# Second half's low weight parts by rows in two buffers; the first residue's tables in the weights' raw buffer

## The chip, the cores and the metric

The kernel runs on one core of a Trainium2 chip. The metric is the device time of one execution in microseconds (us); lower is better. The engines are TensorE (PE, and PEld for its weight loads), VectorE (DVE), ScalarE (ACT), GpSimd (POOL) and SyncE (SP, which here only issues DMAs).

## The reference

One block of a network on 2048 tokens of 1024 channels: a normalisation, a projection, a mixer, and a mixture of experts. The mixer's columns are half a long convolution done by Fourier transforms and half a two-dimensional Fourier transform. The part around the change:

```python
def fourier_mixer(u):
    B, L, _ = u.shape
    ug = u.astype(jnp.float32).reshape(B, L, N_FOURIER_GROUPS, HEAD_DIM)
    y = jnp.fft.fftn(ug, axes=(1, 3), norm='ortho').real
    return y.reshape(B, L, D_FOURIER)
...
    k_f = jnp.fft.rfft(k, n=2 * L, axis=0)
    u_f = jnp.fft.rfft(u, n=2 * L, axis=1)
    return jnp.fft.irfft(u_f * k_f[None], n=2 * L, axis=1)[:, :L]
```

## The kernel before

Products in float32 are made of three products of shorter numbers: each operand is cut into a high and a low part, and high by high, high by low and low by high are summed. The high part is a rounded copy (made on ScalarE), the low part is the operand minus the high part (made on VectorE).

The change lies in one stage, between about 400 and 620 us. Two kinds of work are mixed there.

**Fourier columns.** The 512 Fourier columns of the projection are made in two halves of 256 columns (h = 0 and 1). `fourier(h, i, ...)` makes the tile of 128 tokens number i of a half: 24 matmuls of 256 columns, three for each of the eight blocks d of 128 input channels. The normalised tokens, cut, are `hhi` and `hlo`, and stay in SBUF; the half's weights, cut, are `wh` and `wl`. 16 tiles by two halves by 24 are 768 matmuls. `fweights(h)` loads the half's weights from `Wp` by groups g of 128 columns into the raw buffer (tag `wraw`, one buffer, 4 KB of each partition) and cuts them with `cutg`. `wh` has two buffers (tag `whl`), `wl` one.

**Residues.** The long convolution's spectra are multiplied residue by residue: 32 calls of `residue(n)`. Each loads two tiles (`yl`, from `YK` and `YZ`), cuts them (`yh` on ACT; the low part of the first on POOL, of the second on DVE), makes the products K and U with the tables `sk` and `su`, multiplies them (`ks`, `t1`, `t2` on DVE), cuts the product (`ph` on ACT, `pl` on DVE), makes `zp` with the table `si` and stores it. That is 9 matmuls of 512 columns (12 for residue 0, which has tables of its own). Residues are counted from 0 here.

The calls are written one after the other (six Fourier tiles, six residues, and then a loop over h and i with residues between), and a scheduler decides the order on each engine. Each engine works its list off in that order. After the last tile of the second half the sums and differences of mirrored rows (`pair`, `fold`) and the next transforms (`bins`) follow; `h5` and `mid` are one row of 512 numbers for the middle frequency, `r0` the first rows for `reverse`.

Of the kernel before, what the change touches and what calls it, by code (L numbers as in the profile page):

```python
# [9 lines left out]
F32 = mybir.dt.float32  # L10
F32R = mybir.dt.float32r
# [192 lines left out]
def build(tc, I, out, dbg=None, upto=99):  # L204
# [4 lines left out]
    with es:  # L209
# [65 lines left out]
        with ExitStack() as e1, ExitStack() as e2:  # L275
# [388 lines left out]
            def fweights(h):  # L664

                wh = wp.tile([P, 8, 256], F32R, tag="whl", bufs=2, name="wh")
                wl = wx.tile([P, 8, 256], F32R, tag="wl", bufs=1, name="wl")
                for g in range(2):
                    wr = wp.tile([P, 8, P], F32, tag="wraw", bufs=1, name="wr")
                    S.dma_start(wr, Wp[2 * h + g])  # L670
                    cutg(wh[:, :, P * g:P * g + P], wl[:, :, P * g:P * g + P], wr)
                fw[h] = wh, wl

            def fourier(h, i, wh, wl, pm, dst=None):
# [3 lines left out]
                for d in range(8):  # L678
                    for a, b in ((hhi, wh), (hhi, wl), (hlo, wh)):
                        T.matmul(pm, a[q][:, d, P * o:P * o + P], b[:, d, :], start=n == 0, stop=n == 23)  # L680
                        n += 1
# [3 lines left out]
                if h and i in (12, 4):  # L685

                    rt = wx.tile([P, 256], F32, tag="rt", bufs=2, name="rt")
                    A.copy(rt, pm)
                    A.copy(h5[i // 12][:, 256:512], pm[0:1])
                    rts[i // 12] = rt  # L690
                    return
# [31 lines left out]
            ufirst(15)  # L723
            wh, wl = fw.pop(0)
            for i in range(NFIRST):
# [25 lines left out]
            def prod(o, w, xh, xl):  # L751

                for n, (a, b) in enumerate(((0, xh), (0, xl), (1, xh))):
                    T.matmul(o, w(a), b, start=n == 0, stop=n == 2)

            def residue(n):
# [6 lines left out]
                if n == 0:  # L763

                    for x in range(2):
                        prod(kp[x], lambda a: sk[:, r, a, P * x:P * x + P], kh, kl)
                    for x in range(2):
                        prod(up[x], lambda a: su[:, r, a, 64 - 64 * x:192 - 64 * x], uh, ul)
                    for x in range(2):
# [3 lines left out]
                else:  # L773

                    kp, up = kp[0], up[0]
                    prod(kp, lambda a: sk[:, r, a, 64:192], kh, kl)
                    prod(up, lambda a: su[:, r, a, 64:192], uh, ul)
                    lo, hi = slice(0, 64), slice(64, P)
# [11 lines left out]
                zp = ps.tile([P, DH], F32, tag="Z", bufs=2, name="zp")  # L790
                prod(zp, lambda a: si[:, r, a, :], ph, pl)
                zs = fp.tile([P, DH], F32, tag="zs", bufs=2, name="zs")
# [5 lines left out]
            def j0(i, h):  # L798
                return res < min(NT * h + i + 8, 32)
# [21 lines left out]

            rts, r0, h5 = {}, {}, {}

            def reverse(k):
# [48 lines left out]
            for h in range(2):  # L873
                if h:
                    wh, wl = fw.pop(h)
                for i in range(NT):
# [7 lines left out]
                    if h and i in (13, 14):  # L884
                        reverse(i - 13)
                    while j0(i, h):
                        residue(res)
                        res += 1
                        if res == 32:
# [14 lines left out]

                            x = wp.tile([P, 2, 512], F32, tag="wraw", bufs=1, name="h5")
                            for k in range(2):
                                h5[k] = x[0:1, k]
                                S.dma_start(h5[k][:, 0:256], RM[1 - k][3][0:1, 0:256])
                            lg = gp.tile([P, NT, 36], F32, name="lg")
                            lst = gp.tile([P, 2, 5, NE], F32, name="lst")  # L910
                            x = lg.rearrange("p a b -> p (a b)")
                            for k in range(2):
                                r0[k] = x[0:1, 256 * k:256 * k + 256]
                            jm = lst.rearrange("p a b c -> p (a b c)")[:, 0:P]
# [84 lines left out]
        with ExitStack() as e3:  # L999
# [82 lines left out]
            with tc.tile_pool(name="fo", bufs=1, side="right", reuse_waits="tile") as fo:  # L1082
# [8 lines left out]

                mid = fo.tile([1, 512], F32, name="mid")
                V.tensor_tensor(v4(mid[:, 0:264]), v4(h5[0])[:, :, 0:66], v4(h5[1])[:, :, 0:66], op=ALU.add)
                V.tensor_tensor(v4(mid[:, 264:512]), v4(h5[0])[:, :, 66:128], v4(h5[1])[:, :, 66:128], op=ALU.subtract)

# [899 lines left out]
```

## Time and profile before

| | us |
|---|---|
| median of 3 runs (lowest, highest) | 1671.64 (1668.62, 1673.2) |
| the profiled execution: time, span | 1675.47, 1673.7 |
| PE busy in the span | 1574.7 (94%) |
| DVE busy | 1192.6 (71%) |
| ACT busy | 1031.0 (62%) |
| POOL busy | 438.7 (26%) |

The span is what the hardware profiler saw of one execution; the time has what lies around it too. The busy time of PE counts pipelined matmuls whose ends are modelled, so where it works back to back the distance from start to start says more than the duration. The granted clock of TensorE is a share of full speed: 1.00 is 2.4 GHz, 0.50 is 1.2 GHz.

### The profile page before, as it was taken

The page shows a single profiled execution, that of the slowest core. Times are in us where ns is not written, and L with a number is a line of the kernel's source. Part 1 is how long each engine was busy: PE and PEld are TensorE (multiplying, and loading weights), DVE is VectorE, ACT ScalarE, POOL GpSimd, SP SyncE. Part 2 cuts the span into 40 slices and gives each one's busy share as a digit, 9 for nine tenths or more (in the row PEclk, how much of TensorE's full clock was granted, in tenths as well). Part 3 has the DMA queues.
Part 4 walks back from the last instruction along what each step waited for, and adds up shares of the span by engine and source line. Part 5 has one row for each costly group of instructions (what it writes and reads, how often), then busy time and mean ns, then how long its engine had stood idle before and what let it go on. Part 6 is the DMA issues. An engine that isn't in the chain of part 4 may idle for free.

```text
span 1673.7 us, 27233 instructions
## 1 busy us (share of the span) xinstructions
PE 1574.7 (94%) x8995; PEld 1200.8 (72%) x8995; DVE 1192.6 (71%) x2162; ACT 1031.0 (62%) x1746; POOL 438.7 (26%) x515
## 2 busy tenths in 40 slices
PE   7999999999998999999999999999999999999992
PEld 5767776778887787876666567777777777777740
DVE  7667756533499966555877877888878888888825
ACT  8445667555698844414444467777777777777732
POOL 0202444332233220103434331222222222221112
PEclk9999999999998999999999999999999999999996
DMA  7245677699765587668778689999999999999997
GB/s 265 66 133 156 191 214 217 189 312 256 212 197 189 176 257 232 203 222 229 230 225 320 227 315 337 337 353 361 343 325 338 351 369 340 333 340 349 378 383 281
DMA packets 202447, 449.77 MB, mean 269 GB/s; under 512 B 27037, under 2 KB 83066, under 8 KB 201280
## 3 DMA queue, kind: packets, MB, share of 16 engines
q1 hardware_dynamic: 129176, 316.25, 53.5%
q0 software_dynamic: 39568, 106.07, 22.4%
q10 hardware_dynamic: 33560, 25.69, 4.7%
q8 instruction: 72, 1.18, 0.3%
q14 instruction: 71, 0.58, 0.1%
HBM read 346.05 MB, written 103.17 MB: 268 GB/s over the span
## 4 chain that ended last, share of the span: by engine, by line
PE 73%; DVE 11%; ACT 5%; DMA 4%; issue 3%; POOL 1%; ACTq 0%; DVEq 0%; POOLq 0%; SPq 0%
PE pa L1722 20%; PE py L1815 10%; PE psm L323 9%; PE psd L1055 8%; PE po L1738 4%; PE pm L680 3%; PE po L1754 2%; PE pstr L1685 2%; PE pa L1719 1%; DMA xt<-in_x 1%; POOL acc L513 1%; PE psEO L1075 1%; PE psm L680 1%; PE pstr L1779 1%; PE pseo L1138 1%
## 5 line engine op out<-in xcount | busy, mean ns | idle before, releaser
L1538 DVE TENSOR_TENSOR l<-w,h 128x1024 fp32r<-128x1024 f32 x352 | 425.7, 1223 | 80.0 <-ACT h L1537 60.4
L1537 ACT CAST h<-w 128x1024 fp32r<-128x1024 f32 x352 | 368.9, 1049 | 106.9 <-PE pa L1722 75.2
L323 PE MATMUL psm<-hhi,wt 128*128 128x512 f32 x768 | 249.9, 396 | 0.7 <-ACT hhi L425 0.5
L1722 PE MATMUL pa<-h,xh 128*128 128x512 f32 x464 | 185.6, 400 | 0.2 <-issue 0.2
L1722 PE MATMUL pa<-l,xh 128*128 128x512 f32 x464 | 181.9, 392 | 0.0
L1722 PE MATMUL pa<-h,xl 128*128 128x512 f32 x464 | 181.6, 391 | 0.0
L323 PEld LDWEIGHTS psm<-hhi,wt 128*128 128x128 f32 x768 | 144.7, 189 | 35.9 <-issue 4.0
L323 PE MATMUL psm<-hlo,wt 128*128 128x512 f32 x384 | 151.7, 395 | 0.4 <-DVE hlo L426 0.2
L987 POOL DMA_INDIRECT xg<-XR,gia x30 | 45.9, 1529 | 295.0 <-PE pstr L1685 154.9
L1722 PEld LDWEIGHTS pa<-h,xh 128*128 128x128 f32 x464 | 87.0, 188 | 30.9 <-issue 12.0
L1722 PEld LDWEIGHTS pa<-h,xl 128*128 128x128 f32 x464 | 87.1, 188 | 20.2 <-DVE xl L1690 0.4
L1722 PEld LDWEIGHTS pa<-l,xh 128*128 128x128 f32 x464 | 87.1, 188 | 18.4 <-issue 0.4
L1815 PE MATMUL py<-l,sh 128*128 128x512 f32 x240 | 98.6, 411 | 0.0
L1815 PE MATMUL py<-h,sh 128*128 128x512 f32 x240 | 97.6, 407 | 0.7 <-ACT sh L1783 0.7
L1815 PE MATMUL py<-h,sl 128*128 128x512 f32 x240 | 96.3, 401 | 0.0
L323 PEld LDWEIGHTS psm<-hlo,wt 128*128 128x128 f32 x384 | 72.8, 189 | 16.6 <-DVE hlo L426 1.0
L1758 POOL DMA_INDIRECT X<-yo,sib x18 | 37.2, 2064 | 166.0 <-DVE l L1538 110.9
L748 POOL TENSOR_TENSOR yl<-yl,yh 128x512 fp32r<-128x512 f32 x32 | 48.6, 1522 | 108.2 <-ACT yh L747 82.8
L1738 PE MATMUL po<-w,xot 128*32 128x256 f32 x1152 | 66.9, 381 | 0.0
L513 POOL TENSOR_TENSOR acc<-ab,acc 128x512 f32<-128x512 f32 x32 | 48.2, 1507 | 69.0 <-ACT ab L512 67.8
L347 ACT COPY u<-psm 128x512 f32<-128x512 f32 x48 | 28.1, 586 | 53.0 <-PE psm L323 52.7
L680 PE MATMUL pm<-wh,hhi 128*128 128x256 f32 x208 | 59.9, 289 | 0.8 <-ACT wh L309 0.8
(495 smaller groups left out, 3655.8 us busy)
## 6 DMA issues: line engine op xcount, KB each, us to landing
w<-in_w_gate SPq DMA_DIRECT2D x128, 512.0 KB
w<-in_w_up SPq DMA_DIRECT2D x128, 512.0 KB
w<-in_w_down SPq DMA_DIRECT2D x120, 512.0 KB
xt<-in_x SPq DMA_DIRECT2D x31, 512.0 KB
de<-in_c_decay SPq DMA_DIRECT2D x32, 256.0 KB
YK<-yk ACTq DMA_DIRECT2D x32, 256.0 KB
z<-zT POOLq DMA_DIRECT2D x32, 256.0 KB, 5.9
YZ<-yz SPq DMA_DIRECT2D x64, 128.0 KB
```

Source lines behind the costliest of these rows:

```text
L323: T.matmul(pm, wt[:, a, d, :], b[q][:, d, :], start=n == 0, stop=n == 23)
L513: G.tensor_tensor(KS["acc"], ab, KS["acc"], op=ALU.add)
L680: T.matmul(pm, a[q][:, d, P * o:P * o + P], b[:, d, :], start=n == 0, stop=n == 23)
L748: e.tensor_tensor(yl, y, yh, op=ALU.subtract)
L987: G.indirect_dma_start(xg_[e], None, XR, bass.IndirectOffsetOnAxis(ap=ga[:, e:e + 1], axis=0))
L1055: T.matmul(pd, a[:, c, :], b[:, c, 512 * h:512 * h + 512], start=n == 0, stop=n == 11)
L1537: cuts.append(A.copy(h, raws[n]))
L1538: V.tensor_tensor(l, raws[n], h, op=ALU.subtract)
L1722: T.matmul(pa[m], x[:, 4 * k + c, :], y[:, f], start=d == 0 and q == 0, stop=d == 7 and q == 2)
L1738: T.matmul(po_[e][32 * j:32 * j + 32, 256 * m:256 * m + 256], xoT[e][:, b % 2, 2 * k + b // 2, :], w[:, 256 * j:256 * j + 256], start=b == ...
L1758: G.indirect_dma_start(X4, bass.IndirectOffsetOnAxis(ap=sib[:, d:d + 1], axis=0), yo, None, compute_op=ALU.add)
L1815: T.matmul(py[i], x[:, c, :], y[:, f], start=c == 0 and q == 0, stop=c == 3 and q == 2)
```

## The change

- `fweights(h)` loads the weights by rows (blocks d 0 to 3, then 4 to 7, of both column groups) and no longer by column groups: four DMAs of 256 KB in place of two of 512 KB. High parts: the same 16 casts. Low parts: blocks 0 to 3 go into a buffer `wl` that now has two (4 KB each), and are made with the load; blocks 4 to 7 go into one buffer `wm` (4 KB), and are made by `rest()`, which runs where the half begins. The low parts' memory grows from 8 to 12 KB of each partition.
- The tables of residue 0 (`t0`) lie in the weights' raw buffer until residue 0 is done; those of the other residues have half-size tiles. Three table DMAs on POOL's queue become nine, five of them into `t0`.
- `cs1` (tables of the next stage) takes the raw buffer after the weights; `h5` and `r0` take a buffer of `wl`.
- `mid` is made in two steps per half (`middle`), in the memory of `lg`, and no longer after the stage.

```diff
@@ -664,20 +664,41 @@
                 wh = wp.tile([P, 8, 256], F32R, tag="whl", bufs=2, name="wh")
-                wl = wx.tile([P, 8, 256], F32R, tag="wl", bufs=1, name="wl")
-                for g in range(2):
-                    wr = wp.tile([P, 8, P], F32, tag="wraw", bufs=1, name="wr")
-                    S.dma_start(wr, Wp[2 * h + g])
-                    cutg(wh[:, :, P * g:P * g + P], wl[:, :, P * g:P * g + P], wr)
-                fw[h] = wh, wl
+
+                wls = [wx.tile([P, 4, 256], F32R, tag="wl", bufs=2, name="wl")]
+
+                def low(j):
+                    for d in range(4):
+                        for g in range(2):
+                            sl = slice(P * g, P * g + P)
+                            V.scalar_tensor_tensor(wls[j][:, d, sl], wr[:, g, d, :], g1[:, 4 * j + d:4 * j + d + 1],
+                                                   wh[:, 4 * j + d, sl], op0=ALU.mult, op1=ALU.subtract)
+
+                for j in range(2):
+                    wr = wp.tile([P, 2, 4, P], F32, tag="wraw", bufs=1, name="wr")
+                    for g in range(2):
+                        S.dma_start(wr[:, g], Wp[2 * h + g][:, 4 * j:4 * j + 4, :])
+                    for d in range(4):
+                        for g in range(2):
+                            A.activation(wh[:, 4 * j + d, P * g:P * g + P], wr[:, g, d, :], AF.Copy,
+                                         scale=g1[:, 4 * j + d:4 * j + d + 1])
+                    if j == 0:
+                        low(0)
+
+                def rest():
+                    wls.append(wx.tile([P, 4, 256], F32R, tag="wm", bufs=1, name="wm"))
+                    low(1)
+                    return wh, wls
+
+                fw[h] = rest
...
@@ -733,11 +754,17 @@
-            su = fp.tile([P, 2, 2, 192], F32R, name="su")
-            sk = fp.tile([P, 2, 2, 256], F32R, name="sk")
-            si = fp.tile([P, 2, 2, P], F32R, name="si")
-            for x, n in ((su, "c_su"), (sk, "c_sk"), (si, "c_si")):
-                G.dma_start(x, I[n].rearrange("x p h c -> p x h c"))
+
+            t0 = wp.tile([P, 1024], F32R, tag="wraw", bufs=1, name="t0")
+            su = [[t0[:, 192 * a:192 * a + 192] for a in range(2)]]
+            sk = [[t0[:, 384 + 256 * a:640 + 256 * a] for a in range(2)]]
+            si = [[t0[:, 896:1024], fp.tile([P, P], F32R, name="si0")]]
+            for x, n, w in ((su, "c_su", 192), (sk, "c_sk", 256), (si, "c_si", P)):
+                y = fp.tile([P, 2, w], F32R, name=n)
+                G.dma_start(y, I[n][1])
+                for a in range(2):
+                    G.dma_start(x[0][a], I[n][0, :, a])
+                x.append([y[:, a] for a in range(2)])
...
+            def middle(h):
+                x, y = (h5[k].rearrange("p (g c) -> p g c", g=2) for k in range(2))
+                g = slice(2 * h, 2 * h + 2)
+                V.tensor_tensor(v4(mid[:, 0:264])[:, g], x[:, :, 0:66], y[:, :, 0:66], op=ALU.add)
+                V.tensor_tensor(v4(mid[:, 264:512])[:, g], x[:, :, 66:128], y[:, :, 66:128], op=ALU.subtract)
...
                 if h:
-                    wh, wl = fw.pop(h)
+                    wh, wl = fw.pop(h)()
...
+                    if h and i == 14:
+                        middle(1)
...
-                            css = {1: [fq.tile([P, 2, 2, 2, P], F32R, name="cs1")]}
+                            css = {1: [wp.tile([P, 2, 2, 2, P], F32R, tag="wraw", bufs=1, name="cs1")]}
...
-                            x = wp.tile([P, 2, 512], F32, tag="wraw", bufs=1, name="h5")
+                            x = wx.tile([P, 4, 256], F32, tag="wl", bufs=2, name="h5")
```

The scheduler's lists move in three places. The number after a name is the buffer's, not part of the code.

**VectorE, where the second half's low parts are cut.** Before (`wl` of the second half from its two raw loads, among the operations of residues 16 and 17):

```order
L782 TENSOR_TENSOR ks_5314<-U_5313,ks_5314 128x512
L310 SCALAR_TENSOR_TENSOR wl_4938<-wr_4939,vecs_89,wh_4937 128x128 x8
L789 TENSOR_TENSOR pl_5264<-ks_5249,ph_5263 128x512
L783 SCALAR_TENSOR_TENSOR ks_5314<-U_5313,ks_5314 64x512
L748 TENSOR_TENSOR yl_5438<-yl_5438,yh_5437 128x512
L784 TENSOR_TENSOR ks_5314<-U_5313,ks_5314 64x512
L782 TENSOR_TENSOR ks_5379<-U_5378,ks_5379 128x512
L785 TENSOR_TENSOR ks_5314<-ks_5314 128x512
L783 SCALAR_TENSOR_TENSOR ks_5379<-U_5378,ks_5379 64x512
L310 SCALAR_TENSOR_TENSOR wl_4938<-wr_4957,vecs_89,wh_4937 128x128 x4
L784 TENSOR_TENSOR ks_5379<-U_5378,ks_5379 64x512
L310 SCALAR_TENSOR_TENSOR wl_4938<-wr_4957,vecs_89,wh_4937 128x128 x4
```

After the change, at about the same place (`wm`, from residue 19 on):

```order
L674 SCALAR_TENSOR_TENSOR wm_5672<-wr_4969,vecs_89,wh_4948 128x128
L816 TENSOR_TENSOR pl_5464<-ks_5449,ph_5463 128x512
L811 TENSOR_TENSOR ks_5515<-U_5514,ks_5515 64x512
L674 SCALAR_TENSOR_TENSOR wm_5672<-wr_4969,vecs_89,wh_4948 128x128
L812 TENSOR_TENSOR ks_5515<-ks_5515 128x512
L809 TENSOR_TENSOR ks_5581<-U_5580,ks_5581 128x512
L810 SCALAR_TENSOR_TENSOR ks_5581<-U_5580,ks_5581 64x512
L816 TENSOR_TENSOR pl_5530<-ks_5515,ph_5529 128x512
L811 TENSOR_TENSOR ks_5581<-U_5580,ks_5581 64x512
L674 SCALAR_TENSOR_TENSOR wm_5672<-wr_4969,vecs_89,wh_4948 128x128
L812 TENSOR_TENSOR ks_5581<-ks_5581 128x512
L674 SCALAR_TENSOR_TENSOR wm_5672<-wr_4969,vecs_89,wh_4948 128x128 x2
```

The block of eight and the two of four are gone: eight cuts (`wl`) now stand singly among residues 3 to 11, eight (`wm`) among residues 19 to 22.

**ScalarE, where the second half's high parts are cut.** Before, the first eight stand ahead of the residues (the other eight in one block at residue 18):

```order
L309 ACTIVATE wh_4937<-wr_4939,vecs_89 128x128 x6
L694 COPY rt_4354<-psm_4329 128x256
L309 ACTIVATE wh_4937<-wr_4939,vecs_89 128x128
L694 COPY rt_4382<-psm_4357 128x256
L747 CAST yh_4487<-yl_4488 128x512
```

After the change none stands there; the first two are among the casts of residue 4 and the copies of residue 3:

```order
L774 CAST yh_4615<-yl_4616 128x512
L774 CAST yh_4620<-yl_4621 128x512
L774 CAST yh_4652<-yl_4653 128x512
L815 CAST ph_4567<-ks_4553 128x512
L774 CAST yh_4657<-yl_4658 128x512
L683 ACTIVATE wh_4948<-wr_4950,vecs_89 128x128 x2
L807 COPY ks_4627<-K_4625 64x512
```

All 16 of the second half now stand among residues 3 to 12. Their first load stands on SP's list behind the loads of residue 4 and waits until residue 0 has left the raw buffer.

**TensorE, residues 4 to 7** (`pm` is a Fourier tile). Before:

```order
L754 MATMUL K_4725<-yh_4715,sk_4482 128x512
L754 MATMUL K_4725<-yl_4716,sk_4482 128x512
L754 MATMUL K_4725<-yh_4715,sk_4482 128x512
L754 MATMUL zp_4634<-pl_4631,si_4483 128x512
L754 MATMUL zp_4634<-ph_4630,si_4483 128x512
L680 MATMUL pm_5144<-wl_3994,hhi2_117 128x256
L680 MATMUL pm_5144<-wh_3993,hlo2_121 128x256
L680 MATMUL pm_5144<-wh_3993,hhi2_117 128x256
```

After the change:

```order
L781 MATMUL K_4773<-yh_4763,c_sk_4490 128x512
L781 MATMUL K_4773<-yl_4764,c_sk_4490 128x512
L781 MATMUL K_4773<-yh_4763,c_sk_4490 128x512
L781 MATMUL zp_4682<-ph_4678,c_si_4494 128x512
L781 MATMUL zp_4682<-pl_4679,c_si_4494 128x512
L781 MATMUL zp_4682<-ph_4678,c_si_4494 128x512
L781 MATMUL U_4774<-yh_4768,c_su_4486 128x512
L781 MATMUL U_4774<-yl_4769,c_su_4486 128x512
```

No Fourier matmul stands between the residues' there any more. Counted over the whole list, the 768 Fourier matmuls stand so (from the end of the `zp` of one residue to that of another):

| Fourier matmuls | before | after |
|---|---|---|
| up to the end of residue 0 | 152 | 152 |
| residues 1 to 3 | 44 | 40 |
| residues 4 to 7 | 63 | 0 |
| residues 8 to 16 (residue 8, residue 9) | 125 (14, 15) | 148 (15, 11) |
| residues 17 to 22 | 96 | 93 |
| residues 23 to 31 | 172 | 218 |
| behind residue 31 | 116 | 117 |
| behind residue 28 | 185 | 214 |
| residue matmuls behind the end of residue 28 | 15 | 21 |

The lists of TensorE after this stage are the same but for line numbers.

## Rows read from the trace of the kernel before

**Rows 1.** Windows: busy time of each engine (instructions), granted clock, DMA share, GB/s

```profile
500.00:520.00 20.00, 19.46 (x112) 16.49 (x111) 19.41 (x28) 19.07 (x36) 9.08 (x5) 1.00 0.65 208
522.00:528.00 6.00, 1.59 (x6) 0.83 (x5) 5.88 (x12) 3.97 (x8) 3.25 (x3) 0.88 0.87 276
528.00:536.00 8.00, 7.22 (x26) 6.01 (x26) 6.21 (x15) 4.99 (x13) 1.54 (x1) 0.50 0.50 171
600.00:620.00 20.00, 19.06 (x147) 17.76 (x147) 10.29 (x27) 5.73 (x14) 9.42 (x13) 1.00 0.91 284
```

**Rows 2.** Timeline of DVE: start, duration, operation, idle time before it and releaser

```profile
509.12 0.69 DVE L789 TENSOR_TENSOR pl<-ks,ph 128x512 fp32r<-128x512 f32 x1
...
513.48 0.69 DVE L789 TENSOR_TENSOR pl<-ks,ph 128x512 fp32r<-128x512 f32 x1
...
521.40 3.20 DVE L310 SCALAR_TENSOR_TENSOR wl<-wr,vecs,wh 128x128 fp32r<-128x128 f32 x8
...
531.35 1.22 DVE L310 SCALAR_TENSOR_TENSOR wl<-wr,vecs,wh 128x128 fp32r<-128x128 f32 x4 [1.70 <-ACT wh L309]
...
533.32 1.14 DVE L310 SCALAR_TENSOR_TENSOR wl<-wr,vecs,wh 128x128 fp32r<-128x128 f32 x4
...
606.01 0.43 DVE L838 TENSOR_TENSOR rr<-rr,rr 128x264 f32<-128x264 f32 x1 [6.26 <-DMA rr<-RM,mir]
```

**Rows 3.** Timeline of PE, the same columns

```profile
414.52 0.60 PE L367 MATMUL pst<-ident,cv 128*128 128x128 f32 x4
...
449.70 0.40 PE L754 MATMUL zp<-ph,si 128*128 128x512 f32 x1
...
517.54 0.39 PE L754 MATMUL zp<-ph,si 128*128 128x512 f32 x1
517.76 0.28 PE L680 MATMUL pm<-wh,hlo 128*128 128x256 f32 x1
517.88 0.28 PE L680 MATMUL pm<-wh,hhi 128*128 128x256 f32 x1
...
518.91 0.40 PE L754 MATMUL zp<-ph,si 128*128 128x512 f32 x1
...
522.23 0.28 PE L680 MATMUL pm<-wh,hlo 128*128 128x256 f32 x1
525.25 0.50 PE L754 MATMUL zp<-pl,si 128*128 128x512 f32 x1 [2.74 <-DVE pl L789]
...
527.66 0.79 PE L754 MATMUL U<-yh,su 128*128 128x512 f32 x1 [1.67 <-DVE ks L784]
...
532.17 0.41 PE L680 MATMUL pm<-wh,hlo 128*128 128x256 f32 x1
532.39 0.41 PE L680 MATMUL pm<-wh,hhi 128*128 128x256 f32 x1
...
537.43 0.39 PE L754 MATMUL zp<-ph,si 128*128 128x512 f32 x1
...
588.13 0.40 PE L754 MATMUL zp<-ph,si 128*128 128x512 f32 x1
...
611.41 0.69 PE L828 MATMUL rev<-lg,ident 1*128 1x256 f32 x2 [0.94 <-issue]
...
617.34 0.28 PE L680 MATMUL pm<-wh,hlo 128*128 128x256 f32 x1
```

**Rows 4.** Timeline of ACT, the same columns

```profile
514.20 1.18 ACT L780 COPY ks<-K 64x512 f32<-64x512 f32 x2 [0.26 <-DVE pl L789]
...
530.91 2.44 ACT L309 ACTIVATE wh<-wr,vecs 128x128 fp32r<-128x128 f32 x8 [0.95 <-DMA wr<-Wp]
```

**Rows 5.** Timeline of POOL, the same columns

```profile
403.70 1.17 POOL L551 DMA_DIRECT2D z<-zT  x2
409.07 0.21 POOL L353 COPY u<-u 128x1 f32<-128x1 f32 x1 [4.20 <-ACT u L347]
```

**Rows 6.** Waits of PE from 900 us to the end: total, times, longest

```profile
PE pstr L1779 <- DVE s L1727: 3.8, 1, 3.8
```

More of the change, by code (lines that the diff above doesn't have):

```diff
@@ L678, in fourier @@
                 for d in range(8):
-                    for a, b in ((hhi, wh), (hhi, wl), (hlo, wh)):
-                        T.matmul(pm, a[q][:, d, P * o:P * o + P], b[:, d, :], start=n == 0, stop=n == 23)
+                    for a, b in ((hhi, wh[:, d, :]), (hhi, wl[d // 4][:, d % 4, :]), (hlo, wh[:, d, :])):
+                        T.matmul(pm, a[q][:, d, P * o:P * o + P], b, start=n == 0, stop=n == 23)
                         n += 1
@@ L688, in fourier @@
                     A.copy(rt, pm)
-                    A.copy(h5[i // 12][:, 256:512], pm[0:1])
+                    A.copy(h5[i // 12], pm[0:1])
                     rts[i // 12] = rt
@@ L723, in build @@
             ufirst(15)
-            wh, wl = fw.pop(0)
+            wh, wl = fw.pop(0)()
             for i in range(NFIRST):
@@ L765, in residue @@
                     for x in range(2):
-                        prod(kp[x], lambda a: sk[:, r, a, P * x:P * x + P], kh, kl)
+                        prod(kp[x], lambda a: sk[r][a][:, P * x:P * x + P], kh, kl)
                     for x in range(2):
-                        prod(up[x], lambda a: su[:, r, a, 64 - 64 * x:192 - 64 * x], uh, ul)
+                        prod(up[x], lambda a: su[r][a][:, 64 - 64 * x:192 - 64 * x], uh, ul)
                     for x in range(2):
@@ L775, in residue @@
                     kp, up = kp[0], up[0]
-                    prod(kp, lambda a: sk[:, r, a, 64:192], kh, kl)
-                    prod(up, lambda a: su[:, r, a, 64:192], uh, ul)
+                    prod(kp, lambda a: sk[r][a][:, 64:192], kh, kl)
+                    prod(up, lambda a: su[r][a][:, 64:192], uh, ul)
                     lo, hi = slice(0, 64), slice(64, P)
@@ L903, in build @@
                                 G.dma_start(css[1][0][:, c], I["c_ldft"][1][:, c, :, 0:2])
-                            x = wp.tile([P, 2, 512], F32, tag="wraw", bufs=1, name="h5")
+                            x = wx.tile([P, 4, 256], F32, tag="wl", bufs=2, name="h5")
                             for k in range(2):
-                                h5[k] = x[0:1, k]
-                                S.dma_start(h5[k][:, 0:256], RM[1 - k][3][0:1, 0:256])
+                                h5[k], r0[k] = x[0:1, k], x[0:1, 2 + k]
+                                S.dma_start(h5[k], RM[1 - k][3][0:1, 0:256])
                             lg = gp.tile([P, NT, 36], F32, name="lg")
                             lst = gp.tile([P, 2, 5, NE], F32, name="lst")
-                            x = lg.rearrange("p a b -> p (a b)")
-                            for k in range(2):
-                                r0[k] = x[0:1, 256 * k:256 * k + 256]
+                            mid = lg.rearrange("p a b -> p (a b)")[0:1, 0:512]
+                            middle(0)
                             jm = lst.rearrange("p a b c -> p (a b c)")[:, 0:P]
@@ L1090, in build @@
                 S.dma_start(altr, I["c_altr"])
-                mid = fo.tile([1, 512], F32, name="mid")
-                V.tensor_tensor(v4(mid[:, 0:264]), v4(h5[0])[:, :, 0:66], v4(h5[1])[:, :, 0:66], op=ALU.add)
-                V.tensor_tensor(v4(mid[:, 264:512]), v4(h5[0])[:, :, 66:128], v4(h5[1])[:, :, 66:128], op=ALU.subtract)
                 def pseo():
```

2 lines of the change are left out of this document (1 added, 1 removed).

## The prediction

> **What bounds the kernel now.** I read the windows of the stage first, then the timelines of its engines, and last what comes behind it. In a steady stretch of the stage VectorE is busy 19.41 of 20 us and ScalarE 19.07 [rows 1]; from one `pl` of VectorE to the next is 513.48 − 509.12 = 4.36 us, and that is what a residue takes [rows 2]. ScalarE is nearly as full: it waits 0.26 us in a residue, for VectorE [rows 4]. TensorE's 19.46 us in the same window are durations that overlap. From start to start a residue's matmul takes 0.22 us and a Fourier matmul 0.12 [rows 3], so nine of the one and the 14 or 15 of the other that stand with it come to 3.7 to 3.8 us. So here VectorE sets the pace, ScalarE follows close behind, and TensorE has over half a microsecond to spare per residue. Once the residues are done it turns round: from 600 to 620 us VectorE is busy 10.29 us and TensorE works through [rows 1].
>
> The reader is to see one hole as well. At 522.23 us TensorE has issued its last matmul of the first half that it can, and waits 2.74 us for `pl` and then 1.67 us for `ks` [rows 3]. Both stand behind the eight low cuts that VectorE makes from 521.40 to 524.60; the other eight wait for ScalarE's casts at 530.91, which waited for the second raw load [rows 2, 4]. TensorE's clock was granted at 0.88 over 522 to 528 us, while the engine was busy 1.59 of 6 us, and at 0.50, its lower level, over the eight us behind that [rows 1]; a Fourier matmul then takes 0.22 us in place of 0.12 [rows 3]. The hole is 4.4 us of waiting and half of the 7.2 us that it then works at the low clock, about 8 us. That would be the gain if TensorE alone set the pace.
>
> **What the hole costs now.** Residue 15 ends with its `zp` at 518.91 us, residue 17 at 537.43, residue 28 at 588.13 [rows 3]. At 4.36 us a residue, with the sixteen low cuts of 3.20 + 1.22 + 1.14 = 5.6 us [rows 2] on top, residue 28 would end at 518.91 + 13 × 4.36 + 5.6 = 581.2. So 7.0 us are lost: 4.2 by residue 17 (18.5 − 8.7 − 5.6), 2.7 in the eleven residues after it (50.7 − 48.0), where nothing was cut any more. Behind residue 28 the list leaves 185 Fourier and 15 residue matmuls, 185 × 0.12 + 15 × 0.22 = 25.5 us; the last Fourier matmul starts at 617.34 and is through at 617.46, that is 588.13 + 0.22 + 25.5 + 3.6. The 3.6 us are the reversals between, 0.94 of them a wait [rows 3].
>
> **The change, step by step.**
>
> *Low parts (removes the hole).* The same sixteen operations of 128 by 128, cut singly: 5.6 us of VectorE as before, since blocks of four cost 0.29 to 0.31 us each and the block of eight 0.40 [rows 2]; singles lie between these ends, 4.6 and 6.4 us. They take the same time from the bound engine, but no one is queued behind a block, and the first tile of the second half needs only what is made long before. Gain: the 4.2 us lost by residue 17.
>
> *Order of TensorE (gives most of it back).* The Fourier tiles have moved back: none in residues 4 to 7 (63 before), 218 and not 172 in the last nine, and 214 Fourier and 21 residue matmuls behind residue 28. That is 214 × 0.12 + 21 × 0.22 = 30.3 us, 4.8 more than before, in a stretch where TensorE is the one that works through. The 2.3 us or so of each residue that TensorE has free in residues 4 to 7 are not used.
>
> *High parts.* Eight more casts of 2.44 / 8 = 0.31 us [rows 4] come into the residues; all sixteen now lie in the first thirteen, 4.9 us, and ScalarE has 13 × 0.26 = 3.4 us free there. I take the difference, 1.5 us, as lost; the ends are 0 (VectorE's own cuts give it time) and 4.9. The first load is issued when residue 0 has left the raw buffer, a few us after 449.70 [rows 3], and the first casts stand at residue 4; if it is late, ScalarE waits, and VectorE behind it. I count this in the 4.9.
>
> *Tables of residue 0.* Five more loads are issued by POOL, at 0.58 us each (1.17 for two) 2.9 us, ahead of the halo copy that stood at 409.07 [rows 5]. The copy feeds VectorE and then the transposes at 414.52 [rows 3]: the 5.4 us between cover it. Uncovered it would cost 2.9 us. The tables arrive 30 us before residue 0 needs them.
>
> *Middle row, `cs1`, `h5`, `r0`.* Four small adds in place of two, of 0.43 us each at most (the nearest row is an add of 264 columns [rows 2]). The first two stand where VectorE then waits 6.26 us for the mirrored rows [rows 2]; without that cover 0.9 us. In the new list more matmuls lie between a reversal and the load of `r0`, so I drop the 0.94 us wait [rows 3]; if it stays, that is the cost.
>
> **The sum.** After: residue 28 at 581.2 + 0.22, plus 30.3 behind it, plus 2.7 for the reversals, is 614.4 us if nothing is lost. Before it is 617.46, so at best 3.1 us are gained at the old start of the stage. Against that stand the losses. Those of the steady part stay, 2.7 us as after residue 17: there, too, VectorE and TensorE were both full, and now they are from residue 8 on. With the 1.5 us of ScalarE, 4.2 us. Net 1.1 us slower; the ends are 3.1 faster (no loss) and 8 us slower (4.9 for ScalarE, the 2.7, 0.9 for the adds, and 2.9 for POOL). The value nearer to the middle, +0.5, seems likeliest to me, because single cuts may cost 1.0 us less than blocks. Behind the stage TensorE's list is the same and it waits for no DMA: the longest wait after 900 us is 3.8 us, for VectorE [rows 6], so a shift of the stage carries to the end. The profiled execution took 1675.47 us, so 1676.0 by this sum; it lies 3.8 above the median of 1671.64, and against that the forecast is **1672 us**. No change of less than 0.3%, 5 us, can be told from none here.
>
> **The rivals.**
>
> *Faster.* TensorE sets the pace more than I think, or the first fifteen residues run clean. They took 518.91 − 449.70 = 69.2 us [rows 3] where 15 × 4.36 are 65.4: 3.8 us lost. With fewer Fourier matmuls in the way this could be saved, and with no loss later the gain is 3.1 + 3.8 = 6.9 us; the whole hole would be 8. That gives 1664 to 1666. For it: residues 4 to 7 have nothing between them. Against it: in the steady rows TensorE is not what VectorE waits for. It decides once less than 2 us are lost over the whole stage.
>
> *Slower: the clock falls in residues 4 to 7.* TensorE there has 9 × 0.22 = 2.0 us of work in each 4.36 us, in pieces of three matmuls with waits between. In the one case of this stage the clock fell after the engine had been busy 1.59 of 6 us [rows 1], so the new stretch lies between that and the full one, and the trace does not decide. At the low level residue 8 (15 Fourier matmuls) takes 9 × 0.44 + 15 × 0.22 = 7.3 us and residue 9 (11) 6.4, both over 4.36: VectorE stands 2.9 + 2.0 = 4.9 us, and all behind it is later. With the +0.5 that is 1677; if the stalls of ScalarE come on top, 1680. It decides if the low clock lasts into residue 9.
>
> The Trainium skill, "TensorE: Matmul & The Clock Gate", section "A second HAM failure mode: psum-queue depth-cycling", tells of a kernel in which short idles between groups of matmuls were frequent enough that the clock went back and forth between its two levels. By that rule this rival would be the likely case and the sum 4.9 us higher; by the rows, where the clock stayed at 1.00 with idle gaps in every residue of the steady stretch, it would not. No run so far shows a stretch of residues alone.
>
> **How the numbers follow.** The trade as summed, 1668 to 1676: 0.65. Faster, at 1664 to 1666: 0.14. Slower, at 1677 to 1680: 0.21. The range reaches into both rivals, 1665 to 1679; a tenth is left out on either side or less. Faster by over 0.3% (under 1666.6): 0.14; within: 0.65; slower (over 1676.7): 0.21.
>
> **What would show it.** In the new profile: no wait of TensorE for `pl` or `ks` of over 1 us where the second half begins; residues 4 to 7 at about 4.4 us each, with TensorE busy about half; residue 28 ending within 3 us of 585; from there 33 us to the last Fourier matmul, not 29. If residue 28 ends before 582 the gain is real; if the granted clock is below 1.00 between 465 and 495 us, the slower rival holds. The forecast is wrong if TensorE's later tiles do not cost what they are counted at, or if the stage behind it does not take the shift over.

## The result and the profile after

The changed kernel takes 1682.89 us (median of 7 runs, 1678.78 to 1688.78); before, 1671.64 in the same comparison. The ratio is 1.0065, with a 95% interval of 1.0046 to 1.0085: slower by 11 us (8 to 14). The prediction said 1672, 1665 to 1679. The ratios, here and below, leave out three executions of the experiments (one each of e1, e3 and e13) that took over 100 us longer than the others of their kernel.

The profiled execution took 1682.22 us, its span is 1680.4. The profiled execution of before took 1675.47 us, which is 3.8 over its median, so the two profiles show under 7 of the 11 us. The stage, from the first `K` to the last Fourier matmul, is 183.1 us long (439.69 to 622.80); before it was 175.1 (442.24 to 617.34). Behind it come 1057.6 us, before 1056.4. So 8.0 us were lost in the stage. The stage begins 2.6 us earlier than in the profile of before; in other profiles below it begins between 438.9 and 443.7, so lengths are compared, not ends.

Windows of the stage after the change (columns as in rows 1):

```profile
440.00:460.00 20.00, 17.53 (x90) 14.08 (x89) 16.99 (x22) 16.07 (x30) 7.16 (x5) 1.00 0.60 191
460.00:480.00 20.00, 15.50 (x47) 8.77 (x45) 19.50 (x30) 19.29 (x38) 5.93 (x5) 0.83 0.56 170
480.00:500.00 20.00, 17.88 (x97) 14.29 (x98) 19.30 (x30) 18.92 (x36) 5.73 (x5) 1.00 0.62 195
500.00:520.00 20.00, 17.88 (x99) 15.17 (x97) 16.90 (x23) 17.17 (x36) 5.32 (x4) 0.91 0.62 190
528.00:536.00 8.00, 7.23 (x46) 6.18 (x44) 7.81 (x11) 6.76 (x14) 4.34 (x3) 1.00 0.65 184
540.00:560.00 20.00, 17.83 (x97) 15.17 (x96) 17.62 (x30) 15.68 (x29) 5.89 (x6) 0.91 0.63 204
600.00:620.00 20.00, 20.00 (x155) 18.55 (x153) 12.00 (x31) 7.25 (x16) 8.23 (x12) 1.00 0.75 235
```

The reader sees two things. The hole of 528 to 536 us is gone: clock 1.00 and 46 matmuls where there were 26 [rows 1]. And from 460 to 480 us TensorE starts 47 matmuls; VectorE and ScalarE are as full as ever, so the residues go on at their pace with no Fourier matmul between them. From 600 us on TensorE is busy without a gap.

TensorE's timeline after the change: the first `K`, the last `zp` of residues 0, 3, 7, 8, 16, 28 and 31, and the last Fourier matmul:

```profile
439.69 0.40 PE L781 MATMUL K<-yh,t 128*128 128x512 f32 x1
446.41 0.39 PE L781 MATMUL zp<-ph,si 128*128 128x512 f32 x1
463.54 0.40 PE L781 MATMUL zp<-ph,c_si 128*128 128x512 f32 x1
482.21 0.39 PE L781 MATMUL zp<-ph,c_si 128*128 128x512 f32 x1
486.59 0.39 PE L781 MATMUL zp<-ph,c_si 128*128 128x512 f32 x1
528.71 0.39 PE L781 MATMUL zp<-ph,c_si 128*128 128x512 f32 x1
588.58 0.39 PE L781 MATMUL zp<-ph,c_si 128*128 128x512 f32 x1
606.16 0.40 PE L781 MATMUL zp<-ph,c_si 128*128 128x512 f32 x1
622.80 0.28 PE L701 MATMUL pm<-wh,hlo 128*128 128x256 f32 x1
```

Before the change, the first `K` and the last `zp` of residues 3 and 7 (the others are in [rows 3]):

```profile
442.24 0.39 PE L754 MATMUL K<-yh,sk 128*128 128x512 f32 x1
465.73 0.39 PE L754 MATMUL zp<-ph,si 128*128 128x512 f32 x1
484.10 0.40 PE L754 MATMUL zp<-ph,si 128*128 128x512 f32 x1
```

From such rows, for this and other profiles, in us and (in brackets) Fourier matmuls by each kernel's list. e3, e9 and e12 are experiments of the next section.

| | before | after | e9 | e3 | e12 |
|---|---|---|---|---|---|
| first `K` to residue 0 | 7.46 | 6.72 | 7.07 | 6.72 | 7.35 |
| residues 1 to 3 | 16.03 (44) | 17.13 (40) | 16.02 (40) | 17.00 (46) | 16.53 (44) |
| residues 4 to 7 | 18.37 (63) | 18.67 (0) | 22.20 (0) | 20.54 (61) | 18.37 (63) |
| residues 8 to 16 | 41.50 (125) | 46.50 (148) | 41.35 (137) | 38.40 (124) | 39.21 (131) |
| residues 17 to 28 | 62.53 (199) | 59.87 (214) | 59.93 (232) | 60.81 (193) | 53.50 (186) |
| residue 28 to the last Fourier matmul | 29.21 | 34.22 | 32.55 | 30.56 | 32.85 |
| the stage | 175.10 | 183.11 | 179.12 | 174.03 | 167.81 |

Residues 4 to 7 take the same 18.4 to 18.7 us with 63 Fourier matmuls between them and with none. Their 63 × 0.12 = 7.6 us of TensorE's work have moved behind, and nothing was saved where they stood.

Why they moved is seen in ScalarE's timeline. Tile 7's last matmul is at 462.52 us, but of the two PSUM buffers of the Fourier tiles the first is emptied only at 482.02 us and the second at 486.26, behind casts of `wh` and the residues' work:

```profile
472.22 1.28 ACT L683 ACTIVATE wh<-wr,vecs 128x128 fp32r<-128x128 f32 x4
...
482.02 0.38 ACT L715 COPY rt<-pm 128x256 f32<-128x256 f32 x1
```

The casts of the second half are written in the code ahead of tile 6. While they could run before the residues, they were in nobody's way. Now that their load waits for residue 0 they stand among the residues, and the copies of the tiles wait behind them.

### The profile page after: what moved, and what is told of

Read it like the earlier page. It is cut to its first block, busy times and chain, and to the rows that moved or that the text cites. A ratio compares the mean times of both kernels' runs of the same rounds, so it can differ in the third digit from the quotient of the medians.

```text
span 1680.4 us, 27259 instructions
## 1 busy us (share of the span) xinstructions
PE 1573.8 (94%) x8995; PEld 1196.1 (71%) x8995; DVE 1199.5 (71%) x2164; ACT 1032.1 (61%) x1746; POOL 436.1 (26%) x521
## 4 chain that ended last, share of the span: by engine, by line
PE 70%; DVE 11%; DMA 7%; ACT 5%; issue 4%; POOL 2%; SPq 1%; ACTq 0%; POOLq 0%; DVEq 0%
PE pa L1753 19%; PE py L1846 10%; PE psd L1089 8%; PE psm L323 8%; PE po L1769 4%; PE pm L701 2%; PE po L1785 2%; PE pstr L1716 2%; PE pa L1750 1%; POOL acc L513 1%; DMA cs<-in_c_ldft 1%; PE psm L701 1%; PE pstr L1810 1%; PE psEO L1109 1%; PE pseo L1169 1%
## 5 line engine op out<-in xcount | busy, mean ns | idle before, releaser
L1753 PEld LDWEIGHTS pa<-l,xh 128*128 128x128 f32 x464 | 87.1, 188 | 18.4 <-issue 0.4
L775 POOL TENSOR_TENSOR yl<-yl,yh 128x512 fp32r<-128x512 f32 x32 | 44.9, 1408 | 118.3 <-ACT yh L774 104.7
L701 PE MATMUL pm<-wh,hlo 128*128 128x256 f32 x208 | 59.3, 285 | 0.0
```

The lines of the kernel that those rows point to most:

```text
L701: T.matmul(pm, a[q][:, d, P * o:P * o + P], b, start=n == 0, stop=n == 23)
L775: e.tensor_tensor(yl, y, yh, op=ALU.subtract)
L1753: T.matmul(pa[m], x[:, 4 * k + c, :], y[:, f], start=d == 0 and q == 0, stop=d == 7 and q == 2)
```

## The experiments

Ratios are to the kernel before on the same chip, with the 95% interval. Theory A: the Fourier matmuls that left residues 4 to 7 are paid for later. The rivals B to E are told in the expectations.

| | ratio | median us (before there) |
|---|---|---|
| after the change | 1.0065 (1.0046 to 1.0085) | 1682.89 (1671.64) |
| e1 hold | 1.0054 (1.0032 to 1.0075) | 1680.91 (1674.83) |
| e2 tables alone | 1.0107 (1.0092 to 1.0123) | 1691.08 (1674.83) |
| e3 spread, early last cuts | 1.0004 (0.9991 to 1.0017) | 1675.19 (1674.83) |
| e4 spread | 1.0034 (1.0021 to 1.0047) | 1680.20 (1674.83) |
| e5 hold two | 1.0044 (1.0022 to 1.0066) | 1681.67 (1673.80) |
| e6 filler | 1.0056 (1.0036 to 1.0076) | 1683.69 (1673.80) |
| e7 e3 with lead 7 | 1.0005 (0.9989 to 1.0022) | 1676.21 (1673.80) |
| e8 before with lead 7 | 1.0040 (1.0028 to 1.0052) | 1681.76 (1673.80) |
| e9 hold again | one run | 1681.37 (1674.66) |
| e10 rows alone | 1.0094 (1.0076 to 1.0111) | 1691.72 (1674.66) |
| e11 short buffers | 1.0137 (1.0116 to 1.0158) | 1699.58 (1674.66) |
| e12 no second low | 0.9963 (0.9949 to 0.9978) | 1668.39 (1674.66) |
| e13 spread, cuts with casts | 1.0026 (1.0009 to 1.0043) | 1677.69 (1673.64) |
| e14 behind 31 | 1.0075 (1.0052 to 1.0098) | 1685.57 (1673.64) |

**e1 and e9, the emptied residues alone.**

```diff
+ x = T.matmul(pm, ...)                  # tile 8 of the first half, its first matmul
+ tc.add_manual_dep(x.ins, zps[7].ins.name, ORDER_ONLY, reason="order")   # last zp matmul of residue 7
```

> The kernel before, with one thing added: the first matmul of Fourier tile 8 is held in TensorE's list until residue 7's last matmul, so that residues 4 to 7 stand alone, as after the change; nothing else is edited, the block cuts of the second half stay. Theory A (the Fourier matmuls that no longer stand in residues 4 to 7 are paid for later, since TensorE works nearly through from residue 8 on): 63 x 0.118 = 7.4 us of TensorE's work move behind, so 6 to 9 us slower than before, 1677 to 1681 us. Rival B (VectorE's 4.36 us per residue set the pace to residue 31, TensorE has room for them, and the change lost its time with the single cuts and casts among the residues): within 2 us of before.

> The first run's kernel again, for its profile. Theory A: residues 4 to 7 take as long as before (18 to 20 us for the four) with 63 Fourier matmuls less in them, residues 8 to 31 take 6 to 9 us more than before's 115.7, and the end of residue 31 and the last Fourier matmul are later by that. Rival: the loss lies elsewhere (before residue 4, or behind residue 31).

e1 is 0.54% slower, 9 us (5 to 13; by the table's medians 6), which is theory A's price. e9 is the same kernel run once more for its profile, and there the loss lies elsewhere than theory A said. The stage is 4.0 us longer than before and the span 5.9. Of that 3.8 us are lost in residues 4 to 7 themselves, where the change lost nothing (22.20 us and 18.67), and 3.3 behind residue 28. Residues 8 to 28 came out 2.7 us shorter, not longer: the waits of TensorE in them fell from 9.6 to 5.4 us in sum, and its low clock from 10.2 to 2.1 us, so the matmuls that moved filled a part of the hole. Windows of e9:

```profile
460.00:480.00 20.00, 15.29 (x59) 10.42 (x58) 18.35 (x26) 16.88 (x32) 5.40 (x4) 0.84 0.50 164
480.00:500.00 20.00, 16.71 (x74) 12.52 (x73) 17.86 (x24) 15.29 (x27) 5.16 (x4) 0.81 0.48 156
```

The clock fell in the bare residues here too, and where it was still low at residue 8, with 23 Fourier matmuls, that residue took 6.21 us. At the full clock, residues with 24 take 5.1 us in e9 (residues 25 to 29).

**e5, half of the hold.**

```diff
- tc.add_manual_dep(x.ins, zps[7].ins.name, ORDER_ONLY, reason="order")
+ tc.add_manual_dep(x.ins, zps[5].ins.name, ORDER_ONLY, reason="order")
```

> The kernel before with half of the first run's hold: Fourier tile 8 waits in TensorE's list for residue 5 in place of 7, so only residues 4 and 5 stand alone (35 Fourier matmuls moved behind, not 63). Theory A: 35 x 0.118 = 4.1 us of TensorE's work move behind, 3 to 6 us slower than before, between before and the first run (9 us). Rival B (a change of the list as such costs, whatever its size): as the first run. Rival D (the low clock in residues alone is what costs): 0 to 2 us, if two residues alone do not lower the clock.

0.44% slower, 7 us (4 to 11): with these intervals it can't be told from e1, and no proportion to the matmuls moved is shown; rival B of this run, a cost whatever the size of the move, is not excluded by it. Its windows suggest why the half is dear:

```profile
468.00:472.00 4.00, 3.53 (x8) 1.75 (x7) 3.90 (x5) 2.32 (x5) 2.03 (x2) 0.50 0.48 164
472.00:476.00 4.00, 3.67 (x9) 2.29 (x8) 2.77 (x6) 3.54 (x7) 0.00 (x0) 0.50 0.41 131
476.00:480.00 4.00, 4.00 (x25) 3.71 (x24) 3.94 (x5) 2.85 (x5) 1.29 (x1) 0.85 0.71 188
```

The clock was at 0.50 already in the first of the two bare residues (residue 4, to 470.55 us), and TensorE met its Fourier matmuls again before the clock was back: residue 6, with 21 of them, took 6.66 us, and residues 4 to 7 together 21.8.

**e6, the clock.** K and U of residues 4 to 7 are made twice.

```diff
- prod(kp, ...); prod(up, ...)
+ for _ in range(2 if 4 <= n <= 7 else 1):
+     prod(kp, ...); prod(up, ...)
```

> The kernel after, with the K and U products of residues 4 to 7 made twice (six more matmuls of 512 columns a residue, the second three overwrite the first), so that TensorE is busy about 3.5 of 4.36 us there and keeps its full clock; the Fourier matmuls stay where the change put them from residue 8 on. Theory A: the clock in these residues is not what costs, since they take 4.7 us each with it low as with it high: within 2 us of after, 1681 to 1685. Rival D (the low clock of this stretch costs, by the stalls that it leaves behind): 4 to 6 us faster than after, 1677 to 1679.

As after the change, so rival D gets nothing from it. But the test isn't clean: 19 Fourier matmuls came to stand in residues 4 to 7, and the clock stayed at 1.00 to 478 us and then was 0.50 from 480 to 486, as the filler ended, and residue 8 took 5.5 us. It moved the low clock and did not remove it.

**e2, the tables alone.** The third part of the diff above and nothing else of it:

```diff
- su = fp.tile([P, 2, 2, 192], F32R, name="su")       # sk, si likewise
+ t0 = wp.tile([P, 1024], F32R, tag="wraw", bufs=1, name="t0")
```

> The kernel before, with one part of the change alone: residue 0's tables in the weights' raw buffer (nine table loads); weights by column groups, block cuts and one low buffer as before. In its list, too, residues 4 to 7 have no Fourier matmul between them and 117 stand behind residue 31. Theory A: 6 to 9 us slower than before, 1677 to 1681 us, since this part alone empties residues 4 to 7 (the casts of the second half come behind residue 0 and ahead of the tiles' copies on ScalarE). Rival B (the loss comes from the low cuts and their order): within 2 us of before. Rival C (the five more loads on POOL's queue ahead of the halo copy): 3 us slower, and already there when residue 0 ends.

1.07% slower, 18 us: double of what any theory said. Residues 4 to 7 are empty as expected. Residue 0 ends no later, at 447.43 us where before it is 449.70, so rival C is out; so is rival B, since the cuts stand in blocks here. The stage is 181.2 us long, 6.1 more than before: as in e9 the loss lies in residues 4 to 7 (20.5 us) and behind residue 28 (33.0), and residues 8 to 28 take 104.0 us as before. Another 11.2 us are lost behind the stage, where no theory placed them. Waits of TensorE from 604 to 662 us in e2:

```profile
PE pseo L1143 <- DVE ab L866: 2.4, 2, 2.2
PE pseo L1143 <- DVE hss L1034: 2.2, 1, 2.2
PE pst L1046 <- DVE ya L1038: 1.2, 1, 1.2
PE pseo L1143 <- ACT ab L865: 1.1, 1, 1.1
```

VectorE waits there for the mirrored rows (10.1 us in 4 waits) behind residue 31, TensorE waits for VectorE, and the clock is at 0.71 from 628 to 636 us. The whole change has no such wait: there the first `pseo` starts right behind the last Fourier matmul. Which of its other parts (`h5`, `r0`, `cs1`, or the order of the list) keeps it away was not tried.

**e3, e4 and e13, the residues filled again.** In e3 and e4 the casts of the second half are written between the Fourier tiles (`casts` and `stage` are the loops of `fweights`, cut into steps); in e3 and e13 `rest()` is called ahead of the last residue of the first half.

```diff
+ for _ in range({4: 1, 6: 1, 7: 1, 8: 1, 9: 2, 10: 2, 11: 1, 12: 1, 13: 1}.get(i, 0) if h == 0 else 0):
+     todo.pop(0)()                       # load, four pairs of casts, low cuts; load, four pairs of casts
...
+ if h == 0 and i == 15:
+     nxt = fw.pop(1)()                   # not in e4
```

In e13 two low cuts follow each pair of early casts, and the steps are `{4: 1, 6: 4, 7: 4, 8: 1, 9: 1, 10: 1, 11: 1, 12: 1}`.

> The kernel after, with the second half's high casts written out among the Fourier tiles (tiles 6 to 13, one or two pairs a tile) in place of all ahead of tile 6, and the last low cuts written ahead of the last residue of the first half. Its list has 61 Fourier matmuls in residues 4 to 7 (none after the change), and 192 in place of 214 behind residue 28. Theory A: about 7 us faster than after, 1674 to 1677 us. Rival B: same cuts and casts, so within 2 us of after, 1681 to 1685.

> As the run above, but the last low cuts stay where the change has them, at the start of the second half. Residues 4 to 7 have 61 Fourier matmuls, but residues 18 to 22 only 35 (79 after the change), because the second half's low cuts come late there. Theory A: 63 moved forward and 44 moved back, so 0 to 4 us faster than after, 1679 to 1683, and 4 to 8 us slower than the run above. Rival B: within 2 us of after, and the same as the run above.

> The run with spread casts and early last cuts, with each pair of early low cuts written right behind its pair of casts, and all of the first raw load's by Fourier tile 7, so that the second load can go out earlier. 45 Fourier matmuls in residues 4 to 7 and 73 in residues 13 to 17; 122 behind residue 31, as there. Theory A (the late second load cost that run 3 to 4 us in residues 17 to 22): 2 to 5 us faster than that run and than before, 1669 to 1673. Rival (the cuts and casts among the residues cost what the hole gave): no change against before.

e3 gains 10 us against the change (1.0004 for 1.0065), more than the 7 of theory A, and its stage is 9.1 us shorter. Residues 8 to 28 take 99.2 us and not 106.4, with 45 Fourier matmuls fewer, and behind residue 28 it is 3.7 us shorter, with 22 fewer. Its sixteen low cuts stand mostly singly too and take 7.3 us, so rival B is out: the single cuts are not what costs the change most. e3 moves the casts as well as the Fourier matmuls, and what either is worth by itself is not shown. e4 gains half of that, and e3 is faster than e4 by 5 us: in e4 the matmuls are missing in residues 18 to 22. The window of 460 to 480 us in e3:

```profile
460.00:480.00 20.00, 16.91 (x92) 13.43 (x91) 19.59 (x28) 17.97 (x35) 8.72 (x6) 1.00 0.56 174
```

e13 misses: 0.26% slower than before, where theory A wanted it faster. The late second load is gone, and residues 17 to 22 take 29.6 us for e3's 33.6, the 3 to 4 us that theory A priced. But residues 4 to 7 hold 45 Fourier matmuls only, 8 to 16 take 43.0 us for e3's 38.4, and the clock falls once (0.88 over 510 to 520 us), so the stage is 2.8 us longer than e3's. Neither reaches what e12 shows to be there.

**e10 and e11, the rows without the tables' place.** e10 is the changed kernel with the tables as before; three buffers for the residues' low parts make the room. e11 is the kernel before with this line alone:

```diff
- yl = fp.tile([P, DH], F32R, tag="yl", bufs=5, name="yl")
+ yl = fp.tile([P, DH], F32R, tag="yl", bufs=3, name="yl")
```

> The change's rows and two low buffers, without residue 0's tables in the raw buffer: tables as before, paid for with three buffers in place of five for the residues' low parts. Its list has 65 Fourier matmuls in residues 4 to 7, the second half's early low cuts ahead of the residues, and 70 behind residue 31. Theory A (the rows are good for the hole's 3 to 4 us, the tables' place took it back): 2 to 6 us faster than before and than the run with the short buffers alone. Rival B (single cuts and casts among residues cost what the hole gives): same as before. Rival E (three buffers hold up the next residue's products): slower than before by more than 3 us, and so is the run with the short buffers alone.

> The kernel before with three buffers in place of five for the residues' low parts, and nothing else: the control of the run before this. Its list leaves 89 Fourier matmuls behind residue 31 in place of 116. Theory A: within 3 us of before (the hole stays). Rival E: over 3 us slower.

The buffers cost more than all else, rival E: waits of TensorE over the stage in e10 and in e11 have this at their head (before the change it is 1.1 us in 3 waits). In both, 10 us more are lost behind the stage, where fewer Fourier matmuls stand (see e8).

```profile
PE K L776 <- POOL yl L770: 12.5, 20, 1.0
```

```profile
PE K L754 <- POOL yl L748: 10.0, 18, 0.9
```

But side by side, with the same buffers, the change without the tables' place is worth 1.0137 for 1.0094, 7 us in its favour (the intervals lie apart), the 2 to 6 of theory A or a little more. This is the part that the change is good at.

**e12, the most there is.** The second half's tiles use the first half's low parts.

```diff
- wl = wx.tile([P, 8, 256], F32R, tag="wl", bufs=1, name="wl")
+ wl = fw["l"] if h else wx.tile([P, 8, 256], F32R, tag="wl", bufs=1, name="wl")   # no low cuts for h = 1
```

> The kernel before without the second half's low cuts: its Fourier tiles are made with the first half's low parts (this leaves out 16 cuts, 5.6 us of VectorE, and the wait for them). The most that moving those cuts could give. Theory A, as the prediction counted it: 4.2 us for the hole and 5.6 for the cuts, 8 to 11 us faster than before. Rival (TensorE sets the pace, and the hole alone counts): 7 to 8 us faster. Rival (the mirrored rows behind residue 31 set the end anyway): under 5 us faster.

6 us faster (4 to 9), under theory A's 8 to 11, and the stage is 7.3 us shorter; the two rivals can't be told apart by that. No hole is left: residues 8 to 28 take 92.7 us for 104.0. But 49 Fourier matmuls stand in residue 31, and the end behind residue 28 is 3.6 us longer than before. So 11.3 us off the residues bring 7.3 in the stage: the rest is TensorE's work, which only moves behind.

**e7 and e8, where the residues stand.** In e3's kernel and in the one before:

```diff
- return res < min(NT * h + i + 8, 32)
+ return res < min(NT * h + i + 7, 32)
```

> The run with spread casts and early last cuts, and the residues written one Fourier tile later from tile 6 on (lead 7 in place of 8). Its list leaves 100 Fourier matmuls behind residue 31 and not 122, the 22 stand in the residues. Theory A (what counts is that TensorE has Fourier work wherever VectorE sets the pace): up to 22 x 0.118 = 2.6 us faster than the run without the lead, 1672 to 1675, so 0 to 3 us faster than before. Rival B: VectorE sets the pace to the end and the 22 lie beside it anyway: 2 to 3 us faster too; if instead the residues end later by as much, no change.

> The kernel before with that lead of 7 alone: block cuts, one low buffer, tables apart. 99 Fourier matmuls behind residue 31 in place of 116; residues up to 17 as before. Theory A: the last residues are TensorE's already (1.4 us lost in residues 23 to 31), so the 17 matmuls that move there save at most 17 x 0.118 = 2.0 us: 0 to 2 us faster than before.

Both stages are shorter, 171.1 and 170.5 us, and neither kernel is faster; e8 is slower by 7 us, which theory A did not foretell. (The profiled executions, 1670.83 and 1678.59 us, lie below their medians.) With fewer Fourier matmuls behind residue 31, TensorE runs out of work. In e8 the last Fourier matmul is at 612.01 us, the first products of the next transform follow at once, and then:

```profile
620.53 1.47 PE L1138 MATMUL pseo<-ab,cs 128*128 128x264 f32 x5 [5.27 <-DVE ab L861]
```

This `ab` is made of the mirrored rows, which are loaded behind residue 31: VectorE waits for them 8.2 us in two waits. The product comes 22.6 us behind the end of residue 31, and TensorE's clock is at 0.63 over the 11 us from 621 to 632 us that follow (1.00 from 617.4 to 632 before the change). In e7 the same product comes 19.4 us behind residue 31, with a wait of 1.50. The tail of Fourier matmuls covers this chain where it is long enough; in e2, with 117 of them, the chain took 28.3 us and the tail did not cover it.

**e14, which of the two ends the stage after the change.**
```diff
+ if (h, i, n) == (1, ORDER[10], 0):    # first matmul of the second half's tile 10
+     tc.add_manual_dep(x.ins, zps[31].ins.name, ORDER_ONLY, reason="order")
```

> The kernel after, with Fourier tile 10 of the second half held in TensorE's list until residue 31's last matmul: 23 Fourier matmuls in residue 31 and not 50, 144 behind it and not 117. TensorE's whole work stays as it is. Theory A (TensorE's work sets the end of the stage): residue 31 ends 3 us earlier, the last Fourier matmul as before it, within 2 us of after. Rival (the chain of mirrored rows behind residue 31 sets the end): 3 us faster than after.

Residue 31 ends 1.0 us earlier counted from residue 0, and not 3, and the last Fourier matmul 2.3 us later in the stage (185.4 us); the time can't be told from that after the change, and the 3 us of the mirrored rows don't come. That TensorE's work ends the stage is seen in three rows, the first product of the next transform that waits, before, after and in e14:

```profile
621.21 0.51 PE L1138 MATMUL pseo<-ab,cs 128*128 128x264 f32 x2 [0.26 <-DVE ab L861]
```

```profile
626.67 0.51 PE L1169 MATMUL pseo<-ab,cs 128*128 128x264 f32 x2 [0.24 <-DVE ab L894]
```

```profile
629.21 0.50 PE L1172 MATMUL pseo<-ab,cs 128*128 128x264 f32 x2 [0.24 <-DVE ab L897]
```

Each comes 3.87 us behind its last Fourier matmul (617.34, 622.80 and 625.34), and 21.4, 20.5 and 23.8 us behind residue 31. So it follows the last Fourier tile and not residue 31. VectorE, which makes the mirrored rows' sums, stood still after the change until that tile was done:

```profile
623.16 0.07 DVE L1063 MEMSET hss<- 128x8 f32 x1 [2.37 <-PE pm L701]
```

## Why the prediction was wrong

**Right.** The long waits where the second half begins are gone: residues 16 and 17 take 8.7 us and not 18.5. Residues 4 to 7 take 4.7 us each (4.4 were foretold) with no Fourier matmul between them. Behind residue 28 it is 34.2 us to the last Fourier matmul; 33 were foretold, 29.2 stood before. A shift of the stage carried to the end.

**The step that failed: "Order of TensorE".** It counted the moved matmuls where they stand behind residue 28 (4.8 us; measured 5.0) and took the rest as lying beside VectorE's work, where it put the loss of the steady part at 2.7 us and ScalarE's at 1.5. From the end of residue 0 to that of residue 28 this makes 581.2 + 4.2 − 449.7 = 135.7 us. It took 142.2, and 138.4 before the change. Residues 8 to 28 got 38 more (324 to 362), 38 × 0.12 = 4.6 us, and the time that was thought free did not take them up. Those residues outside the hole (8 to 15 and 18 to 28) took 97.7 us, before 85.5: 42 matmuls more, 5.0 us, and 7.2 us in which TensorE stood or ran slowly: by the trace it waits 9.9 us there, before 4.4, and its clock is low over 6.8 us, before never. The 0.55 us that TensorE had free in a steady residue were free while the matmuls were spread evenly; in clumps of 20 to 25 a residue they take 9 × 0.23 + 24 × 0.12 = 5.0 us, more than the 4.36 of VectorE. That filling the residues again, with the casts spread, gives the time back is shown by e3. That emptying them costs time is shown by e1 and e2, but there, with the hole still in place, residues 8 to 28 did not grow; that the clumps are what made them grow after the change is argued from the residues' times and not tried by itself.

**A term off in size: the single cuts.** They were put at 4.6 to 6.4 us. VectorE's groups by form, 440 to 600 us, after the change and before:

```profile
L674 DVE SCALAR_TENSOR_TENSOR wl<-wr,vecs,wh 128x128 fp32r<-128x128 f32 x8 | 4.4, 545 | 0.2
L674 DVE SCALAR_TENSOR_TENSOR wm<-wr,vecs,wh 128x128 fp32r<-128x128 f32 x8 | 4.2, 532 | 0.2
```

```profile
L310 DVE SCALAR_TENSOR_TENSOR wl<-wr,vecs,wh 128x128 fp32r<-128x128 f32 x16 | 5.6, 409 | 1.7 <-ACT wh L309 1.7
```

8.6 us, 3.0 more than before. The 0.40 us of the block of eight, taken as an upper end, were no price of a block: seven of its cuts took 0.34 or 0.35 us and one 1.35, beside a GpSimd operation (see the last section). The forecast's +0.5 us with the 4.6 and these 3.0 comes to 8.1, and the stage is 8.0 longer; that the sums meet is partly luck, since the high casts aren't measured apart. They did hurt once: five of the second load (1.57 us at 502.17) stand ahead of `ph` on ScalarE, VectorE waits 1.12 us for it, TensorE 1.14 for `yl`, and with the low clock that follows residue 13 takes 9.3 us.

**The rival that named the right side had the wrong cause.** The clock did fall in residues 4 to 7 (0.83 over 460 to 480 us), which the prediction called its sign. But residue 8 took 4.38 us and residue 9 3.71, where 7.3 and 6.4 were priced: the clock was back before the Fourier matmuls were. In e5 and e9 it wasn't, and there it cost. The Trainium skill, "TensorE: Matmul & The Clock Gate", section "A second HAM failure mode: psum-queue depth-cycling", tells of a clock that goes back and forth where TensorE idles shortly between groups of matmuls. The traces agree in part: in the bare residues the clock fell to 0.50 and rose again, once after the change and twice in e9, but after the change no loss is seen behind it (residues 8 and 9 took 8.1 us, before 8.8).

**Left open.** How much of the 7 us of standing in residues 8 to 28 is due to the clumps, how much to ScalarE's casts and how much to the cuts; why residues 8 to 16 grew in e13. No version that does the whole work was found to beat the kernel before: e3 and e7 equal it.

## What to carry to other kernels

A stretch in which TensorE idles at no cost is not free if it held work that belongs elsewhere: count the work that leaves it, and ask of every later stretch whether it has room, not only of the last one. Moving a load behind a buffer that comes free later also moves all work that waits for it, and here its casts came between other tiles and the copies that empty their PSUM buffers. And a tail that looks like work left over may be the cover of a chain of transfers: shortening it by 17 matmuls (e8) cost 7 us.

## What the hardware showed that was not expected

VectorE's operations on SBUF alone stretch when a GpSimd cut runs beside them. VectorE's and GpSimd's timelines after the change:

```profile
488.59 0.33 DVE L674 SCALAR_TENSOR_TENSOR wl<-wr,vecs,wh 128x128 fp32r<-128x128 f32 x1
...
490.32 1.30 DVE L674 SCALAR_TENSOR_TENSOR wl<-wr,vecs,wh 128x128 fp32r<-128x128 f32 x1
```

```profile
490.17 1.30 POOL L775 TENSOR_TENSOR yl<-yl,yh 128x512 fp32r<-128x512 f32 x1 [2.85 <-ACT yh L774]
```

The same cut takes 0.33 us alone and 1.30 beside a `yl` of GpSimd, and ends 0.15 us after that (491.62 and 491.47). Of the 16 cuts the six of over 0.5 us overlap such a `yl`, the ten of 0.33 to 0.36 don't. Of the 93 products of residues 1 to 31 that read PSUM (`ks<-U`) 26 overlap one and none is a fifth longer than the shortest. So a short operation set singly among GpSimd's work can wait as long as GpSimd's operation lasts; the block of eight before the change met it once (one cut of 1.35 us beside the `yl` of 522.21 to 523.66). The Trainium skill, "SBUF — State Buffer", section "SBUF: two separate sides", says that a VectorE operation with two SBUF inputs and a GpSimd operation that reads SBUF exclude each other for a whole instruction; these rows agree.
